# Expert stage of a two-layer trunk: branches placed in the engines' order, row pairs of 8 KB, and a rebuilt last sum

## The chip, the cores and the metric

The kernel runs on one core of one Trainium2 chip. The metric is the device time of one execution in microseconds. Three runs of the kernel before took 1338.13 to 1340.0 us, median 1339.05. All work is in float32; matrix products of "float32r" operands take one pass, those of float32 operands two instructions each in the trace.

## The reference

256 tokens of width 1024 pass an even layer (stick-breaking and differential attention, then a dense SwiGLU) and an odd layer (chunked band attention, then experts). The change touches the experts alone:

```python
logits = (t @ w_router).astype(F32)
top_val, top_idx = lax.top_k(logits, TOP_K)          # 2 of 8
gates = jax.nn.softmax(top_val, axis=-1)
combine = jnp.einsum('tk,tke->te', gates, jax.nn.one_hot(top_idx, N_EXPERTS, dtype=F32))
y = jnp.zeros_like(t)
for e in range(N_EXPERTS):                            # FF width 3584
    y = y + combine[:, e:e + 1] * swiglu(t, we_gate[e], we_up[e], we_down[e])
```

The weights of the eight experts are 8 x 3 x 1024 x 3584 floats, 352 MB.

## The kernel before

Everything up to the router (lines 203 to 790 and the setup from 1144 on) is the same in both kernels. After the router, each expert's rows are gathered by a product with a one-hot matrix (`dispatch`, `Rows.gather`, lines 888 to 914): the first 64 rows of an expert are its **main** rows, rows 65 to 96 its **further** rows. An expert whose count is above 64 is called crowded here; it needs the further rows too. In this input the experts 1, 3, 5 and 7 are crowded (their further products stand in the trace), 0, 2, 4 and 6 are not.

The 3584 columns of an expert are worked off in chunks of 512, 1024, 1024 and 1024 (line 793). For a chunk, `main_cols` (line 916) multiplies the 64 main rows by the gate and then by the up weights, two column halves at a time on the two 64-column halves of the array; `over_cols` (line 926) does the same for 32 further rows, with four column groups on the array's four 32-column parts. `swiglu` evaluates on ScalarE and VectorE, `turn` transposes the activations, `main_down` and `over_down` (lines 946 and 957) multiply by the down weights into sums that last over the expert. At its end `Scatter` splits the sums in a high and a low part (`split_from`), spreads them back to the tokens by a one-hot product (`halves`, `add_over`) and adds them, weighted, to `yx`; the last expert stores `yx`.

The weights arrive in pieces of 1 MB, one DMA each, issued by SyncE (line 801): 42 pieces an expert, four with rows of 2 KB (chunk 512), the others with rows of 4 KB, the down rows as two rows of 4 KB from different halves of the piece. A ring of 19 buffers holds them (7 `raw`, 6 `rawb`, 5 `w`, 1 `hTl`). `feed.more(n)` asks for n new pieces where n old ones have been used; in the chunk loop it stands behind the branch that holds the further products of gate and up (line 1099) and behind the one of the down rows (1111, 1120).

The further products stand in a branch, `arm` (line 1035, `tc.If` at 1041): eight an expert, one for gate and up of each chunk together, one for the down rows of each. All five engines pass every branch. An engine that skips one waits there until its own earlier work is done and then counts up its semaphore for what it left out.

The order on TensorE, ScalarE and VectorE is the traced order, written by `Ordered` (lines 840 to 857) between `begin` and `end`. `arm` ends an order ahead of the branch and begins one behind it, so the branch itself is in no order and the scheduler places it. The product banks: two for gate and up (`mm`), one shared in halves by the further gate and up (`gu`), one for the main down sum, two for the further down sums, two for transposes.

Of the kernel before, what the change touches and what calls it, by code (L numbers as in the profile page):

```python
# [44 lines left out]
DYN = True  # L45
# [3 lines left out]
def kernel(ctx: ExitStack, tc: tile.TileContext, A: dict, out: bass.AP):  # L49
# [27 lines left out]

    def raw_tile():
        pool, tag = ring[0]
        ring.rotate(-1)  # L80
        return pool.tile([P, 4, 512], F32, name=tag)
# [96 lines left out]

    @contextmanager
    def in_order():  # L180
# [8 lines left out]
        for i in traced[start:]:  # L189
            if i.engine in (EngineType.PE, EngineType.Activation, EngineType.DVE):  # L190
                if i.engine in last:
                    tc.add_manual_dep(i, last[i.engine], mybir.DependencyInfo(
                        mybir.DependencyClass.NoSync, mybir.DependencyReason.DATA), reason="in order")
                last[i.engine] = i.name
# [598 lines left out]
    CHUNKS = [(0, 512)] + [(c, 1024) for c in range(512, FFE, 1024)]  # L793

    def cols_piece(w, c0, n, k):

        nk = 2048 // n

        def load():
            r = raw_tile().rearrange("p a b -> p (a b)").rearrange("p (k c) -> p k c", c=n)  # L800
            nc.sync.dma_start(r, w[k * P:(k + nk) * P, c0:c0 + n].rearrange("(kb p) c -> p kb c", p=P))
            return r
        return load

    def rows_piece(w, r0):

        return cols_piece(w, 0, D, r0 // P)

    def pieces_of(e):

        for c, (c0, n) in enumerate(CHUNKS):
            for w in (eg[e], eu[e]):
                for k in range(0, KB, 2048 // n):
                    yield cols_piece(w, c0, n, k)
            if c:
                p0, pn = CHUNKS[c - 1]
                for r in range(p0, p0 + pn, 2 * P):
                    yield rows_piece(ed[e], r)
        c0, n = CHUNKS[-1]
        for r in range(c0, c0 + n, 2 * P):  # L820
            yield rows_piece(ed[e], r)
# [18 lines left out]
    class Ordered:  # L840


        def begin(self):
            self.bb = nc.cur_bb
            self.before = self.bb.bb.instructions[-1] if self.bb.bb.instructions else None

        def end(self):
            assert nc.cur_bb is self.bb
            traced = self.bb.bb.instructions
            start = next((k + 1 for k in reversed(range(len(traced))) if traced[k] is self.before), 0)  # L850
            last = {}
            for i in traced[start:]:
                if i.engine in (EngineType.PE, EngineType.Activation, EngineType.DVE):
                    if i.engine in last:
                        tc.add_manual_dep(i, last[i.engine], mybir.DependencyInfo(
                            mybir.DependencyClass.NoSync, mybir.DependencyReason.DATA), reason="in order")
                    last[i.engine] = i.name

    order = Ordered()

    with ExitStack() as ph:
# [4 lines left out]

        slots = act.tile([P, 2, P], F32, name="slots")
        nc.gpsimd.iota(slots[:, 0].rearrange("p (g s) -> p g s", g=2), pattern=[[0, 2], [1, MAIN]], base=0,
                       channel_multiplier=0, allow_small_or_imprecise_dtypes=True)
        nc.gpsimd.iota(slots[:, 1].rearrange("p (g s) -> p g s", g=GROUPS), pattern=[[0, GROUPS], [1, OV]], base=MAIN,  # L870
                       channel_multiplier=0, allow_small_or_imprecise_dtypes=True)
        slots = slots.rearrange("p a b -> p (a b)")
# [12 lines left out]
        yx = act.tile([P, T, D], F32, name="yx")  # L885
        aos = act.tile([P, 2, 1024 // GROUPS], F32, name="aos")

        def dispatch(e):

            dt = act.tile([P, T, 2 * P], F32R, name="disp")  # L890
            dx = act.tile([P, T, CAP], F32, name="dispx")
            for t in range(T):
                nc.vector.tensor_scalar(dx[:, t], slots[:, MAIN:MAIN + CAP], pos[:, t, e:e + 1], selx[:, t, e:e + 1],
                                        op0=OP.is_equal, op1=OP.mult)
            for t in range(T):
                nc.vector.tensor_scalar(dt[:, t], slots, pos[:, t, e:e + 1], sel[:, t, e:e + 1],
                                        op0=OP.is_equal, op1=OP.mult)
            return dt.bitcast(F32), dx
# [17 lines left out]
        def main_cols(o, rows, tiles, n):  # L916

            h, kb = n // 2, 0
            for r in tiles:
                for i in range(2048 // n):  # L920
                    for k in range(2):
                        mm(o[k * MAIN:(k + 1) * MAIN, 0:h], rows.xg[:, kb, 0:MAIN], r[:, i, k * h:(k + 1) * h],
                           kb == 0, kb == KB - 1)
                    kb += 1

        def over_cols(o, rows, tiles, n):
            h, kb = n // GROUPS, 0
            for r in tiles:
                for i in range(2048 // n):
                    for k in range(GROUPS):  # L930
                        mm(o[k * OV:(k + 1) * OV, 0:h], rows.xg[:, kb, MAIN:CAP], r[:, i, k * h:(k + 1) * h],
                           kb == 0, kb == KB - 1)
                    kb += 1

        def swiglu(a, g, u, w):
            nc.scalar.activation(a[:, 0:w], g[:, 0:w], AF.Silu)  # L936
# [408 lines left out]
```

## Time and profile before

| | us |
|---|---|
| runs (3) | 1338.13, 1339.05, 1340.0 |
| profiled execution, its own time | 1338.82 |
| its span, first to last instruction | 1337.1 |
| TensorE busy | 1285.9 (96%) |
| VectorE, ScalarE busy | 388.2, 322.5 |
| DMA moved | 426.71 MB, 318 GB/s read over the span |
| expert stage, first product to last sum | 464.7 to 1327.5 |

The profile cuts the span in 40 slices of 33 us and gives for each the busy tenths of every engine and of the DMA engines. From slice 15 on the DMA engines are full (9) and TensorE is at 9 or 8; VectorE and ScalarE are nearly idle. TensorE's granted clock is full in all slices but the last. A row of the timeline or of the chain begins with the start and the duration in us; a bracket behind it gives the idle time before and what ended it.

### The profile page before, as it was taken

The numbers are of one execution on the slowest core, as the hardware profiler recorded it, in microseconds if no ns is written. First come the engines' busy times: TensorE is split into PE (matmuls) and PEld (weight loads), VectorE is DVE, ScalarE is ACT, GpSimd is POOL, SyncE is SP. The second block draws the span as 40 slices with busy tenths as digits, with TensorE's granted clock in tenths as the row PEclk, the third lists the DMA queues.
The fourth block names the chain that finished last, engine by engine and source line by source line (L and its number), as shares of the span: only waits on it lengthen the run. The fifth ranks groups of instructions, "written<-read, shape, count | busy, mean of one in ns | idle before, by whom it ended". The sixth has DMA issues, their size and how long they took to land. (4 is left out here: it accounts for less than half of the span.)

```text
span 1337.1 us, 19574 instructions
## 1 busy us (share of the span) xinstructions
PE 1285.9 (96%) x8137; PEld 695.2 (52%) x8137; DVE 388.2 (29%) x738; ACT 322.5 (24%) x593; POOL 10.8 (1%) x34
## 2 busy tenths in 40 slices
PE   9999999999999999999999999999899999989995
PEld 6777888888776833533443433433343344334331
DVE  6965554446788500100110100020010011011002
ACT  7675544445666400000000000000000000000000
POOL 0000000000000000000000000000000000000000
PEclk9999999999999999999999999999999999999998
DMA  9623555556464979999999999999999999999981
GB/s 347 226 73 127 179 194 183 176 175 205 137 202 144 410 292 408 402 409 408 401 408 408 401 408 408 403 407 408 407 396 409 409 394 408 408 386 408 409 346 36
DMA packets 132877, 426.71 MB, mean 319 GB/s; under 512 B 7184, under 2 KB 9872, under 8 KB 132752
## 3 DMA queue, kind: packets, MB, share of 16 engines
q1 hardware_dynamic: 131680, 422.80, 82.0%
q0 software_dynamic: 640, 2.10, 0.7%
q8 instruction: 88, 1.44, 0.4%
q14 instruction: 37, 0.30, 0.1%
q10 hardware_dynamic: 432, 0.07, 0.1%
HBM read 423.89 MB, written 1.05 MB: 318 GB/s over the span
## 5 line engine op out<-in xcount | busy, mean ns | idle before, releaser
L60 PE MATMUL mm<-w,hTh 128*128 128x512 f32 (+2 forms) x968 | 291.4, 444 | 1.5 <-DVE w L141 0.8
L60 PEld LDWEIGHTS mm<-w,hTh 128*128 128x128 f32 (+1 forms) x968 | 153.3, 176 | 63.1 <-issue 27.8
L141 DVE TENSOR_TENSOR w<-raw,w 128x1024 fp32r<-128x1024 f32 (+1 forms) x127 | 153.9, 1214 | 91.0 <-ACT w L140 90.6
L140 ACT ACTIVATE w<-raw 128x1024 fp32r<-128x1024 f32 (+1 forms) x127 | 133.5, 1052 | 86.8 <-PE mm L60 51.3
L60 PE MATMUL mm<-w,hTl 128*128 128x512 f32 x368 | 146.4, 398 | 0.0
L60 PE MATMUL za<-raw,hTh 128*32 128x256 f32 (+2 forms) x1200 | 122.6, 417 | 6.5 <-DMA raw<-in_od_we_down 4.5
L937 DVE TENSOR_TENSOR aos<-za,aos 128x256 f32<-128x256 f32 (+1 forms) x16 | 6.3, 392 | 326.5 <-ACT aos L936 326.5
L60 PE MATMUL za<-rawb,hTh 128*32 128x256 f32 (+2 forms) x896 | 98.0, 434 | 2.7 <-DMA rawb<-in_od_we_down 1.7
L937 DVE TENSOR_TENSOR a<-mm,a 128x512 f32<-128x512 f32 (+1 forms) x31 | 19.6, 631 | 250.2 <-PE mm L60 250.2
L60 PEld LDWEIGHTS za<-raw,hTh 128*32 128x32 f32 (+1 forms) x1200 | 51.3, 118 | 70.6 <-issue 50.3
L944 ACT ACTIVATE hTh<-tr 128x512 f32<-128x512 f32 (+1 forms) x32 | 17.4, 544 | 284.7 <-PE tr L943 284.7
L60 PE MATMUL mm<-raw,hTh 128*64 128x512 f32 (+1 forms) x432 | 83.5, 526 | 1.9 <-DMA raw<-in_od_we_up 1.8
L60 PE MATMUL mm<-w,oTh 128*64 128x512 f32 (+2 forms) x344 | 79.2, 521 | 2.6 <-DMA w<-in_od_we_up 1.7
L60 PEld LDWEIGHTS mm<-w,hTl 128*128 128x128 f32 x368 | 69.4, 188 | 14.7
L60 PE MATMUL za<-w,hTh 128*32 128x256 f32 (+2 forms) x672 | 73.5, 441 | 2.1 <-issue 1.3
L60 PE MATMUL mm<-rawb,oTh 128*64 128x512 f32 (+1 forms) x360 | 70.7, 530 | 4.0 <-DMA rawb<-in_od_we_up 1.9
L60 PE MATMUL mm<-raw,oTh 128*64 128x512 f32 (+1 forms) x320 | 68.7, 565 | 2.5 <-DMA raw<-in_od_we_up 1.7
L60 PEld LDWEIGHTS za<-rawb,hTh 128*32 128x32 f32 (+1 forms) x896 | 39.8, 119 | 56.0 <-issue 40.6
L60 PE MATMUL mm<-rawb,hTh 128*64 128x512 f32 (+1 forms) x296 | 58.6, 539 | 1.8 <-DMA rawb<-in_od_we_gate 1.2
L60 PEld LDWEIGHTS mm<-raw,hTh 128*64 128x64 f32 x432 | 29.9, 136 | 47.6 <-issue 37.8
L60 PEld LDWEIGHTS mm<-w,oTh 128*64 128x64 f32 (+1 forms) x344 | 31.3, 146 | 39.6 <-issue 28.5
L60 PEld LDWEIGHTS za<-w,hTh 128*32 128x32 f32 (+1 forms) x672 | 29.8, 118 | 42.3 <-issue 32.0
(278 smaller groups left out, 1201.6 us busy)
## 6 DMA issues: line engine op xcount, KB each, us to landing
raw<-in_od_we_up SPq DMA_DIRECT2D x44, 1024.0 KB, 18.6
raw<-in_od_we_down SPq DMA_DIRECT2D x42, 1024.0 KB, 18.5
raw<-in_od_we_gate SPq DMA_DIRECT2D x40, 1024.0 KB, 18.5
rawb<-in_od_we_gate SPq DMA_DIRECT2D x38, 1024.0 KB, 18.6
rawb<-in_od_we_down SPq DMA_DIRECT2D x38, 1024.0 KB, 18.4
rawb<-in_od_we_up SPq DMA_DIRECT2D x32, 1024.0 KB, 18.6
w<-in_od_we_up SPq DMA_DIRECT2D x30, 1024.0 KB, 18.5
w<-in_od_we_gate SPq DMA_DIRECT2D x29, 1024.0 KB, 18.2
```

The costliest lines, as they stand in the source:

```text
L60: nc.tensor.matmul(o, lhsT, rhs, start=start, stop=stop, skip_group_check=True)
L140: nc.scalar.activation(hi[:, s], r[:, s], AF.Copy)
L141: nc.vector.tensor_tensor(lo[:, s], r[:, s], hi[:, s].bitcast(F32), op=OP.subtract)
L937: nc.vector.tensor_tensor(a[:, 0:w], u[:, 0:w], a[:, 0:w], op=OP.mult)
L944: nc.scalar.activation(dst[:, 0:w], pt[:, 0:w], AF.Copy)
```

## The change

1. `in_order` takes the place of `Ordered`. It stays open over the whole expert stage, and a branch instruction is put in the order of all three compute engines, where it was traced.
2. There is one branch behind each product: gate and up have one each, so 12 an expert (11 in expert 0, whose first gate product is made earlier, 13 in expert 7). `feed.more` follows each.
3. The gate's and up's banks are three in rotation (`banks`). The further product takes the bank that the next main product will take.
4. The further product of the 512 chunk is made in two groups of 256 columns in place of four of 128 (`groups`).
5. Down rows are loaded as `(p j) c -> p j c`: two neighbouring rows, 8 KB, to a partition. So that the rows match, the transposes read every second column of the activations (`turn`).
6. `turn` of the main activations stands in the middle of a main product, and the gather for the next expert behind the third down branch.
7. In the last expert the main and the further rows are summed in the same four banks (`finish`), behind all down products, and added once.
8. `yx`, the room for the split sums and `dT` are made at the end of expert 0; the activations and further activations have one buffer each; dispatch compares in four smaller steps. The eight counts are read inside the order, all ahead of the first expert.

```diff
@@ in_order
+            branch = "Conditional" in type(i).__name__
+            for engine in COMPUTE if branch else (i.engine,):
+                if engine not in COMPUTE:
+                    continue
+                if engine in last:
+                    tc.add_manual_dep(i, last[engine], mybir.DependencyInfo(
                         mybir.DependencyClass.NoSync, mybir.DependencyReason.DATA), reason="in order")
+                last[engine] = i.name
@@ rows_piece
-        return cols_piece(w, 0, D, r0 // P)
+        def load():
+            r = piece().rearrange("p (j c) -> p j c", j=2)
+            nc.sync.dma_start(r, w[r0:r0 + 2 * P, :].rearrange("(p j) c -> p j c", j=2))
+            return r
@@ products
+        def groups(n):
+            w = max(256, n // GROUPS // 256 * 256 + (256 if n // GROUPS % 256 else 0))
+            return n // w, w
+        def main_cols(o, rows, tiles, n, between=None):
...
+                if between and kb == KB // 2:
+                    between()
         def over_cols(o, rows, tiles, n):
-            h, kb = n // GROUPS, 0
...
+            g, w = groups(n)
+            for kb, r in enumerate(rows_in(tiles)):
+                for k in range(g):
+                    mm(o[k * OV:(k + 1) * OV, 0:w], rows.xg[:, kb, MAIN:CAP], r[:, k * w:(k + 1) * w],
+                       kb == 0, kb == KB - 1)
+        def turn(a, np, w, dst, m):
...
+                    c, j = b + i // 2 * 256, i % 2
+                    nc.tensor.transpose(pt[:, i * P:i * P + np], a[0:np, c + j:c + 2 * P:2], ident[0:np, 0:np])
@@ Scatter
+            def finish(self, aT, dn, n, rv):
+                yy = [split_room() for _ in range(2)]
+                self.split()
+                with arm(rv):
+                    over_down(yo, aT, dn, n, False, True)
+                    for h in range(2):
+                        split_from(yy[h][:, 0], yy[h][:, 1], yo[h])
+                os = [[acc[0], acc[1]], [acc[2], bank("tr")]]
+                for t in range(T):
+                    self.main_sums(os[t], t, rv is not None)
+                with arm(rv):
+                    for t in range(T):
+                        for h in range(2):
+                            self.over_sums(os[t][h], yy[h], t, False)
+                for t in range(T):
+                    for k in range(2):
+                        self.add_to(t, k, os[t][k])
+                        s = slice(k * 512, k * 512 + 512)
+                        nc.sync.dma_start(out[t * P:(t + 1) * P, s], total[0][:, t, s])
@@ arm
-            order.end()
             with tc.If(rv > MAIN):
-                order.begin()
-                yield
-                order.end()
-            order.begin()
+                with in_order():
+                    yield
+        def banks(n, use=True):
+            found = [acc[(at[0] + i) % 3] for i in range(n)]
+            at[0] += n * use
+            return found
@@ expert, chunk loop
+                if not done:
+                    gt = feed.take(KB // max(1, 2048 // n))
+                    g = banks(m)
+                    main_cols(g, rows, gt, n, (lambda: turn_main(0)) if c == 1 else None)
+                a = act.tile([P, 1024], F32, name="a")
+                if not done:
+                    activate(a, g, n)
+                    with arm(rv):
+                        go, = banks(1, False)
+                        over_cols(go, rows, gt, n)
+                        if c == 1:
+                            turn_over(0)
+                        nc.scalar.activation(ao[0:og * OV, 0:ow], go[0:og * OV, 0:ow], AF.Silu)
+                    feed.more(len(gt))
                 if c == 0 and before:
                     before.add(0)
...
+                activate(a, u, n, True)
+                with arm(rv):
+                    uo, = banks(1, False)
+                    over_cols(uo, rows, ut, n)
...
+                    nc.vector.tensor_tensor(ao[0:og * OV, 0:ow], uo[0:og * OV, 0:ow], ao[0:og * OV, 0:ow], op=OP.mult)
+                feed.more(len(ut))
                 if c == 0 and before:
                     before.add(1)
...
                 if c:
+                    down(c - 1, False, lambda: turn_main(c), c)
+            if nxt:
+                nxt.gather(range(0, 4))
+                nxt.gather(range(4, 8))
+            down(len(chunks) - 1, True)
```

## Rows read from the trace of the kernel before

**Rows 1.** The page, span in 40 slices: TensorE and DMA in tenths, GB/s moved

```profile
PE   9999999999999999999999999999899999989995
DMA  9623555556464979999999999999999999999981
GB/s 347 226 73 127 179 194 183 176 175 205 137 202 144 410 292 408 402 409 408 401 408 408 401 408 408 403 407 408 407 396 409 409 394 408 408 386 408 409 346 36
```

**Rows 2.** The chain that ended last: start, duration, what

```profile
1204.96 18.12 DMA w<-in_od_we_up
...
1225.32 7.04 PE za L60 x128
...
1326.91 0.61 DVE yx L998
```

**Rows 3.** Windows, one per expert 0 to 7: columns in the first line

```profile
core 0: us, PE busy (x) PEld busy (x) DVE busy (x) ACT busy (x) POOL busy (x), PEclk, DMA share, GB/s
464.70:545.98 81.28, 79.10 (x396) 30.98 (x396) 6.44 (x18) 4.84 (x9) 0.00 (x0) 1.00 0.91 358
545.98:670.36 124.38, 123.06 (x1068) 52.95 (x1065) 13.93 (x25) 9.27 (x20) 0.00 (x0) 1.00 1.03 407
670.36:758.93 88.57, 83.58 (x429) 32.41 (x427) 8.25 (x15) 5.33 (x10) 0.00 (x0) 1.00 1.03 406
758.93:886.73 127.80, 124.03 (x1068) 52.75 (x1066) 13.92 (x25) 9.27 (x20) 0.00 (x0) 1.00 1.03 406
886.73:977.77 91.04, 84.21 (x429) 32.21 (x427) 8.25 (x15) 5.33 (x10) 0.00 (x0) 1.00 1.02 404
977.77:1107.24 129.47, 125.82 (x1068) 53.29 (x1066) 14.02 (x25) 9.27 (x20) 0.00 (x0) 0.99 1.02 404
1107.24:1197.27 90.03, 83.97 (x428) 32.18 (x425) 8.25 (x15) 5.84 (x11) 0.00 (x0) 1.00 1.02 402
1197.27:1327.60 130.33, 123.55 (x1041) 50.16 (x1041) 15.20 (x24) 9.30 (x21) 0.00 (x0) 0.99 0.81 321
```

**Rows 4.** Windows of the expert stage where the transfers slow down

```profile
470.00:480.00 10.00, 9.22 (x42) 2.96 (x40) 0.13 (x1) 0.98 (x2) 0.00 (x0) 1.00 0.12 36
1190.00:1200.00 10.00, 8.61 (x48) 3.25 (x46) 0.69 (x1) 0.60 (x1) 0.00 (x0) 1.00 0.96 339
```

**Rows 5.** Timeline, SyncE and TensorE at the first branch

```profile
461.72 0.42 SPq L801 DMA_DIRECT2D hTl<-in_od_we_up  x1
469.71 0.42 DVE L1077 TENSOR_TENSOR a<-mm,a 128x256 f32<-128x256 f32 x1 [3.06 <-ACT a L1076]
478.31 0.37 SPq L801 DMA_DIRECT2D raw<-in_od_we_up  x1
478.96 4.91 PE L60 MATMUL mm<-rawb,oTh 128*64 128x512 f32 x21 [0.78 <-PEq L1041]
```

**Rows 6.** Windows, za products only: further products of chunk 512, chunk 1024

```profile
552.10:555.73 3.63, 3.63 (x128) 3.43 (x128) 0.00 (x0) 0.00 (x0) 1.00 1.02 406
571.21:578.26 7.05, 7.05 (x128) 4.06 (x128) 0.00 (x0) 0.00 (x0) 1.00 1.03 407
```

**Rows 7.** Timeline, expert 7: ScalarE evictions and TensorE behind one

```profile
1305.92 0.38 ACT L944 ACTIVATE oTh<-tr 128x256 f32<-128x256 f32 x1 [12.58 <-PE tr L943]
1306.25 0.60 ACT L944 ACTIVATE hTh<-tr 128x512 f32<-128x512 f32 x1
1306.90 1.51 PE L60 MATMUL za<-rawb,hTh 128*64 128x512 f32 x6 [0.75 <-ACT hTh L944]
```

**Rows 8.** Line 1041, the branches, and a usual wait behind a skipped one

```profile
L1041 PEldq COMPARE_BRANCH  x96: 70/176/4692, 473.8 to 1319.0; - x96
692.14 1.94 PE L60 MATMUL mm<-w,oTh 128*64 128x512 f32 x8 [0.16 <-PEq L1041]
```

**Rows 9.** Timeline, the end of expert 7

```profile
1315.05 0.60 ACT L247 ACTIVATE oTl<-zb 128x512 fp32r<-128x512 f32 x1 [8.20 <-PE zb L60]
...
1316.42 0.96 PE L60 MATMUL tr<-oTl,dT 128*128 128x512 f32 x3 [0.15 <-DVE oTl L248]
...
1319.92 1.94 PE L60 MATMUL za<-raw,hTh 128*64 128x512 f32 x8
...
1326.11 1.41 DVE L998 SCALAR_TENSOR_TENSOR yx<-tr,comb,yx 128x512 f32<-128x512 f32 x2 [0.89 <-PE tr L60]
```

**Rows 10.** Weight loads of the transposes in expert 1, by form

```profile
L943 PEld LDWEIGHTS tr<-ident,a 128*128 128x128 f32 x14 | 1.6, 140 | 3.2 <-issue 3.2
```

**Rows 11.** Windows, transfers of 2 KB rows, then of 4 KB rows

```profile
535.00:545.00 10.00, 9.69 (x59) 5.37 (x60) 1.12 (x2) 0.57 (x1) 0.00 (x0) 1.00 1.05 387
560.00:570.00 10.00, 10.00 (x49) 3.27 (x47) 0.00 (x0) 0.87 (x2) 0.00 (x0) 1.00 1.03 410
```

More of the change, by code (lines that the diff above doesn't have):

```diff
@@ L838, in take @@
             return [self.tiles.popleft() for _ in range(n)]
[L840 to L859, printed above, removed]
     with ExitStack() as ph:
@@ L926, in over_cols @@
         def over_cols(o, rows, tiles, n):
-            h, kb = n // GROUPS, 0
[L928 to L936, printed above, removed]
-            nc.vector.tensor_tensor(a[:, 0:w], u[:, 0:w], a[:, 0:w], op=OP.mult)
@@ L1008, in halves, with add_over @@
                 for k in range(2):
                     self.add_to(t, k, os[k])
[L1010 to L1025 removed]
+            def add_over(self, yy):
@@ new lines, in down @@
+            def down(c, final, between=None, turns=None):
+                n = chunks[c]
+                dn = feed.take(n // 256)
+                main_down(y, aTs[0][c % 2], dn, n, c == 0, final, between)
+                if final and last:
+                    s.finish(aTs[1][c % 2], dn, n, rv)
+                    return
+                if final:
+                    s.split()
+                    yy = act.tile([P, 2, 512], F32R, name="a")
+                with arm(rv):
+                    over_down(yo, aTs[1][c % 2], dn, n, c == 0, final)
+                    if turns is not None:
+                        turn_over(turns)
+                    if final:
+                        s.add_over(yy)
+                feed.more(len(dn))
@@ L1058, in expert @@
+            ao = aos
+            for c, n in enumerate(chunks):
                 done = first and not c
+                m = len(parts(n))
+                og, ow = groups(n)
                 gt = []
                 if not done:
[L1061 to L1067 removed]
+                    gt = feed.take(KB // max(1, 2048 // n))
[11 more added lines that the diff above has]
+                    feed.more(len(gt))
@@ L1112, in expert @@
-                was = a
-            n, i = CHUNKS[-1][1], (len(CHUNKS) - 1) % 2
-            dn = feed.take(n // 256)
-            main_down(s.y, aTs[0][i], dn, n, False, True)
-            s.split()
-            with arm(rv):
-                over_down(s.yo, aTs[1][i], dn, n, False, True)
-                s.add_over()
-            feed.more(len(dn))
-            if last:
-                for t in range(T):
-                    s.add(t, True)
+                if c == len(chunks) - 1:
+                    if not total:
+                        total.extend(sums())
+                    s.turn()
@@ L1293 @@
                 nc.vector.tensor_scalar(pos, pos, -float(CAP), None, op0=OP.add)
-                order.begin()
-                rows = Rows(0, rooms[0])
-                rows.gather(range(0, 4))
-                rows.gather(range(4, 8))
-                pieces = Pieces(p for e in range(NE) for p in pieces_of(e))
-                pieces.more(len(ring))
-                experts(rows, pieces, None, None)
-                order.end()
+                with in_order():
+                    rows = Rows(0, rooms[0])
+                    rows.gather(range(0, 4))
+                    rows.gather(range(4, 8))
+                    pieces = Pieces(p for e in range(NE) for p in pieces_of(e))
+                    pieces.more(len(ring))
+                    experts(rows, pieces, None, None)
 _BIG = ("ev_w_in", "ev_w_out", "ev_w_gate", "ev_w_up", "ev_w_down", "od_w_qkv", "od_w_out",
```

294 lines of the change are left out of this document (135 added, 159 removed).

## The prediction, made before the changed kernel ran

> **What bounds the kernel now.** I began with the slices. From slice 15 on the DMA engines are full and TensorE is at 9 or 8 tenths [rows 1]: two resources near their limit. The chain of waits says which one ends last: it follows transfers until 1223.07 us, and from there TensorE's products up to the last addition at 1326.91 [rows 2]. So the stream of weights binds until deep in the last expert, and then the products do. Cutting the stage by expert shows by how much [rows 3]. Expert 1 ran without waiting for the stream: 124.4 us for a crowded expert. A light one has about 83.6 us of products (83.58, 84.21, 83.97 busy). Against these prices the others lost: expert 2 5.0 us, 4 7.4, 6 6.4, 3 3.4, 5 3.6 (5.1 less 1.5 lost at the lower clock level: a mean granted clock of 0.99 is, by its rounding, 0.6 to 1.9 us, and I take a value in the upper half) and 7 3.4 (by its own tail, not in the rows of others). Sum 29.2 us of waiting for transfers. Without it a pair of experts would cost TensorE 124.4 + 83.6 = 208.0; the stream needs 84 pieces x 1.0486 MB at the 408 GB/s of the full slices [rows 1], or 215.9. The stream is the slower one by 8 us a pair.
>
> Where does the stream lose time of its own? In 470 to 480 it moved at 36 GB/s, and at 1190 to 1200 at 339 [rows 4]. The timeline gives the reason of the first: the nineteenth buffer is filled by an issue at 461.72 and the next issue comes at 478.31, since SyncE stands behind the first branch, which TensorE passes just ahead of 478.96 [rows 5]. That branch belongs behind the up product, whose eviction ended at 469.71 + 0.42. The scheduler had put it behind most of the next chunk's gate product.
>
> **The change, part by part,** against the profiled execution (1338.82 us, 0.23 under the median).
>
> *Branches in the order, one behind each product.* SyncE's first issue moves from 478.31 to about 470, so the hole of some 9 us shrinks to about 3: a gain of 6.2. Four later dips of the kind of 1190 to 1200 (17% of 10 us each, with their edges about 1 us) come from pieces freed in lumps behind two branches a chunk; with three they come smaller: about 4. The stream is then 10.2 us ahead. It no longer binds if TensorE's own path is later than it at each expert, and with the additions below it is: expert 7 would start at 1195 or later by the products (see the sum) and at 1197.27 - 10.2 = 1187 by the stream, while the 19 buffers allow a lead of 49 us. So the waits go: **-29.2**. What is late next is TensorE itself: its pair rises to 215.7, level with the stream's.
>
> *Further product of the 512 chunk in two groups.* Gate and up together are 128 instructions on four array parts: 3.63 us in chunk 512 and 7.05 in chunk 1024 [rows 6]. The first are 128 columns wide, the second, of chunk 1024, 256 wide, so 32 steps of four abreast take 0.22 each. The new form has 64 instructions of 256 columns for gate and up together, two abreast, so again 32 steps of 0.22, or 7.05 in place of 3.63: 3.4 for each of four crowded experts, **+13.6**. If two abreast run faster a step than four it is less, down to 0.
>
> *The bank shared by the next main product.* In a crowded expert the up product starts in the bank that the further gate product has just left, so TensorE stands until ScalarE has read it; three such meetings wait for SiLU of 128x256 (0.38, by the eviction of that size [rows 7]) and a gap of 0.1; chunk 1 has an eviction of turned rows ahead of it, 0.38 + 0.38 + 0.1 (before, that eviction's own gap of 0.75 on TensorE stood in expert 7 [rows 7]); chunk 0 is covered by the scatter products. 0.48 + 0.48 + 0.88 = 1.8, x 4 = **+7.2**. Ends: 0, if these products are long enough behind; 4.0 if each also waits for VectorE's multiplication.
>
> *More skipped branches.* Four more an expert. TensorE's usual gap behind a skipped one is 0.16 [rows 8]; that is 0.6. Skipping, ScalarE must pass the branch before the bank counts as free, which I put at the 0.78 that TensorE stood behind the first branch, where ScalarE was passing too [rows 5]; 0.78 - 0.16 on three chunks is 1.9. Together 2.5 in experts 2, 4 and 6, and 2.0 in expert 0, which also reads the eight counts in TensorE's order under the gather (0 to 2.5): **+9.5**. Ends: 0 for banks that are free, 4 x 0.78 = 3.1 a light expert, at the largest gap. What is queued behind these waits: on TensorE every later product, on SyncE the next eight or fewer issues (about 0.4 each [rows 5]), which the 49 us of buffers cover as long as they are full.
>
> *The end.* The gap of 0.75 [rows 7] goes, as turning moves into a product. The serial addition of the further rows, from 1315.05 to the next main product at 1319.92, goes: -4.9 [rows 9]. From the last main product's end (1319.92 + 1.94 = 1321.86) to the last addition's end (1326.11 + 1.41 = 1327.52) there are 5.66; the new tail has the two-step split (0.60 + 0.69), some 0.75 for the first bank's sums, and four additions of 0.7: 4.85, with the other sums beside the additions. -0.8, together **-6.4**. Bounds: -4.9 less all that the bank moves may add, say -3, and -8, if half of the split is covered too. The stores stand on SyncE behind the last weight issue, as now.
>
> *Costed at nothing.* Transposes of every second column: the weight loads of fourteen turned tiles take 0.14 us each, with 3.2 us idle ahead of them, 0.23 each [rows 10]. No row shows a strided one. Were they twice as long, the 28 of an expert would add 0.14 each, which that idle time covers; uncovered it is 3.9 an expert, 31 in all. I take 0. Rows of 8 KB: those of 2 KB moved 387 GB/s and those of 4 KB 410 [rows 11], or 2.71 and 2.56 us a piece, 0.15 less; half of that again, 0.075, over 112 down pieces makes 8.4 us, but for a stream that no longer ends last. Bounds for the stream: no gain, and 8.4; a loss is not excluded by a row, and would eat into the lead of 8 us. The dispatch in four steps, the extra passes on VectorE and ScalarE and the moved gather lie beside TensorE's products, both engines being busy for 5 to 15 of 80 to 130 us, and POOL for none [rows 3]. If a product had to wait for the dispatch, it would be about as long as the first gap, 0.78 [rows 5], once an expert. Behind the last addition 11.3 us remain, as before.
>
> Sum: -29.2 + 13.6 + 7.2 + 9.5 - 6.4 = -5.3. 1338.82 - 5.3 = 1333.5, and 0.23 to the median: **1334**. By expert: 83.3 for expert 0, 129.6 for a crowded one, 86.1 for a light one, so TensorE reaches expert 7 at 464.7 + 83.3 + 3 x 129.6 + 3 x 86.1 = 1195.1, or 1196.6 with the 1.5 of the lower clock level.
>
> The trace shows 96 branch passes on TensorE of 70 to 4692 ns, median 176, and a gap of 0.16 behind a skipped one [rows 8]; the sum goes by that gap. The Trainium skill, page "Runtime: NRT & Kernel Launch", section "Instruction fetch mechanics", says that a taken branch to a target outside the fetched window stops the engine until the target has been fetched, which speaks against four more skips an expert. By that rule each of these skips would cost more than the gap, which is rival C. The trace agrees with it as far as the 4692 ns go, and not in the gaps, which products already queued cover.
>
> **Rivals.** *B, faster by more, the waits for banks are hidden:* 0 in place of 16.7, TensorE's pair is 211.4 and the stream, 10.2 us ahead, sets the time as it did. Expert 7 starts at 1187.1 and takes 130.33 - 3.4 + 3.4 - 6.4 = 123.9; with 11.2 behind it that is 1322, and with seven eighths of the 8 KB gain 1315. For it: ScalarE and VectorE are idle most of the time [rows 3]. Against it: a product that reuses a bank cannot start ahead of its reader. Chance 0.20.
>
> *C, slower, by the branches:* the engine that skips an arm must get the instructions behind it, and TensorE's queue at the gate's new branch is too short to hide that. It decides from about 0.35 us more than forecast at each of 15 new gate branches of the light experts (5.3 us, the forecast's gain). At 0.78 more [rows 5] it is 1333.5 + 11.7 = 1345; at 0.62 more on all 47 branches of the light experts it is 1363. For it: passes of up to 4692 ns [rows 8]. Against it: most gaps in the trace are 0.16. Chance 0.18.
>
> *D, it does not do what it says:* SyncE waits as now, because an engine still reaches the branch late, the hole at 470 to 480 stays at some 36 GB/s, and the stream stays the bound up to expert 7: 1338.8 + 5.2 for its bank waits and wider product - 6.4 for the end = 1337.6, or 1337 to 1339. Against it: the branch is in all three engines' order; for it: SyncE's own issues are bound to none. Chance 0.20.
>
> **How the numbers follow.** The forecast has 0.42, B 0.20, D 0.20, C 0.18. The forecast's own range is 1330 to 1337. A measurement of this kernel tells 0.2% (2.7 us) from no change: faster is B and most of the forecast (0.57), same is D and the forecast's upper end (0.23), slower is C and a little (0.20). The range takes in most of B, all of the forecast and D and the lower part of C: 1321 to 1345.
>
> **What would show it.** In the profile after: the window 470 to 480 well above 36 GB/s and SyncE's first issue near 470; crowded experts at 129 to 130 and light ones at 86, with no wait for a transfer on TensorE after expert 1; the further products of chunk 512 at 7.05 for gate and up; waits of about 0.5 on ScalarE ahead of up products, and rows of 8 KB landing no later than now. Wrong if the chain still runs through transfers to the last expert (B or D, told apart by 470 to 480), or if gaps behind skipped branches near 0.8 add up (C); and the size of the tail is wrong if the last product-to-addition stretch is above 5.7.

## The result: 1.1% slower, with TensorE as the bound of the expert stage

The changed kernel takes 1354.01 us (median of 4 runs, 1352.91 to 1355.44), the kernel before 1339.53 beside it: ratio 1.0109, 95% interval [1.0098, 1.0121]. Its profiled execution spans 1352.1 us against 1337.1, so 15.0 us are to be explained. The forecast was 1334, a gain of 5; its range ended at 1345.

The page of the changed kernel, the span in 40 slices:

```profile
PE   9999999999999999999999999999999999999995
...
DMA  9623555555445999999999999999999999999931
GB/s 350 217 91 128 166 208 184 182 176 190 143 169 205 386 371 407 410 411 411 397 354 413 402 412 413 405 378 399 408 409 412 412 403 368 414 402 412 412 155 37
```

Against [rows 1]: TensorE has a 9 in every slice but the last. The transfers reach 412 to 414 GB/s where they run freely (408 before), and now fall back at places in mid-stage (354, 378, 368): the stream is held up by TensorE. The page's part 4, the chain of waits by engine (it reaches back to 1209.91 us), has no transfer in it, and some pieces of the chain in order of time follow it:

```profile
PE 9%; DVE 0%; ACT 0%; issue 0%; ACTq 0%; DVEq 0%
```

```profile
1237.68 0.36 ACT aos L1147
...
1238.09 7.09 PE za L59 x32
```

In [rows 2] it followed transfers until 1223.07. The piece at 1237.68 is one of the new waits, an up product standing until ScalarE has read the further gate product out of the bank. The windows by expert, columns as in [rows 3]:

```profile
465.65:549.91 84.26, 79.34 (x395) 31.30 (x395) 5.61 (x15) 7.21 (x12) 0.00 (x0) 1.00 0.97 383
549.91:682.15 132.24, 129.18 (x1002) 53.58 (x1003) 14.45 (x27) 9.91 (x21) 0.00 (x0) 0.99 1.01 403
682.15:771.09 88.94, 84.44 (x428) 33.55 (x427) 8.79 (x18) 5.31 (x10) 0.00 (x0) 0.99 1.00 394
771.09:902.70 131.61, 128.54 (x1004) 53.27 (x1004) 14.10 (x27) 9.81 (x21) 0.00 (x0) 1.00 1.01 402
902.70:990.60 87.90, 83.50 (x427) 33.09 (x427) 9.04 (x18) 5.21 (x10) 0.00 (x0) 1.00 1.02 404
990.60:1122.16 131.56, 128.50 (x1002) 53.24 (x1002) 14.05 (x27) 9.91 (x21) 0.00 (x0) 1.00 1.01 403
1122.16:1210.11 87.95, 83.55 (x428) 33.12 (x427) 9.09 (x18) 5.21 (x10) 0.00 (x0) 1.00 1.01 402
1210.11:1338.60 128.49, 125.36 (x978) 50.41 (x978) 12.50 (x20) 9.92 (x21) 0.00 (x0) 1.00 0.70 281
```

In the experts 3 to 6 a light expert (one that is not crowded) takes 87.9 and a crowded one 131.6, so a pair 219.5; the experts 1 and 2 take 132.2 and 88.9 at a mean granted clock of 0.99. Forecast were 86.1, 129.6 and 215.7. Waits for transfers are gone, as forecast: of TensorE's waits in the whole stage one alone is put down to a transfer, 1.45 us ahead of the first product at 465.65, and what stands there in TensorE's queue is the reading of the eight counts:

```profile
L1341 PEldq TENSOR_LOAD <-count x8: 300/307/490, 462.1 to 465.1; - x8
```

The stage from its first product to its last addition still grows from 862.8 us (464.70 to 1327.52) to 872.95 (465.65 to 1338.60). That is 10.1 of the 15.0. The first product comes 0.95 later, and from the last addition to the end of the span there are 13.5 us in place of 9.6: 3.9.

SyncE's first issue and the window 470 to 480 are as forecast, too; the window moved 36 GB/s before [rows 4]:

```profile
470.31 0.37 SPq L824 DMA_DIRECT2D raw<-in_od_we_up  x1
...
470.00:480.00 10.00, 8.27 (x38) 2.63 (x38) 0.42 (x1) 1.36 (x3) 0.00 (x0) 1.00 0.63 226
```

What the new waits are, by the waits of TensorE (what waits, for what, us in total, times, longest), first in the crowded expert 1, then in the light expert 2:

```profile
PE mm L59 <- ACT aos L1147: 1.1, 2, 0.6
PE tr L59 <- DVE a L255: 0.7, 1, 0.7
PE za L59 <- ACT aos L1147: 0.6, 1, 0.6
...
PE mm L59 <- ACTq L1075: 1.5, 2, 0.7
PE tr L59 <- PEq L1075: 0.8, 3, 0.3
PE za L59 <- ACTq L1075: 0.7, 1, 0.7
PE mm L59 <- PEq L1075: 0.7, 2, 0.4
PE za L59 <- PEq L1075: 0.6, 3, 0.3
PE tr L1007 <- PEq L1075: 0.2, 1, 0.2
```

`ACT aos` is the SiLU of the further gate product, three times 0.6. `ACTq L1075` is ScalarE's pass through a skipped branch, three times 0.7, where the up product takes the bank that the skipped arm (the branch's body) would have used. The `PEq` rows, 2.3 us, are TensorE's own passes through skipped branches.

### The profile page after: what moved, and what is told of

It is laid out like the page before. It is cut to its first block, busy times and chain, and to the rows that moved or that the text cites. A ratio compares the mean times of both kernels' runs of the same rounds, so it can differ in the third digit from the quotient of the medians.

```text
span 1352.1 us, 19378 instructions
## 1 busy us (share of the span) xinstructions
PE 1300.4 (96%) x7885; PEld 700.2 (52%) x7885; DVE 389.0 (29%) x750; ACT 324.8 (24%) x593; POOL 10.5 (1%) x33
## 5 line engine op out<-in xcount | busy, mean ns | idle before, releaser
L59 PE MATMUL mm<-w,hTh 128*128 128x512 f32 x736 | 240.0, 400 | 0.5 <-DVE w L143 0.5
L59 PEld LDWEIGHTS mm<-w,hTh 128*128 128x128 f32 x736 | 137.8, 188 | 32.6 <-issue 1.3
L1091 DVE TENSOR_TENSOR a<-mm,a 128x512 f32<-128x512 f32 (+1 forms) x22 | 13.6, 619 | 365.1 <-PE mm L59 169.7
L59 PE MATMUL mm<-raw,xg 128*32 128x256 f32 (+2 forms) x800 | 88.5, 428 | 1.5 <-ACT aos L1147 1.1
L59 PE MATMUL za<-raw,hTh 128*64 128x512 f32 x336 | 78.5, 598 | 0.5 <-PEq L1075 0.5
L59 PE MATMUL za<-rawb,hTh 128*64 128x512 f32 x304 | 69.9, 598 | 0.3 <-PEq L1075 0.3
L59 PE MATMUL mm<-rawb,xg 128*64 128x512 f32 (+2 forms) x440 | 67.8, 486 | 1.2 <-ACT aos L1147 1.2
L59 PEld LDWEIGHTS mm<-raw,xg 128*32 128x32 f32 (+1 forms) x800 | 38.8, 119 | 48.2 <-issue 28.6
L59 PE MATMUL za<-w,hTh 128*64 128x512 f32 x208 | 48.2, 599 | 0.3 <-PEq L1075 0.3
L59 PE MATMUL za<-raw,xg 128*32 128x256 f32 (+2 forms) x352 | 44.3, 449 | 2.1 <-ACT aos L1147 1.8
L59 PE MATMUL mm<-w,xg 128*32 128x256 f32 (+2 forms) x496 | 43.9, 416 | 1.1 <-ACT aos L1147 1.1
```

Source lines behind the costliest of these rows:

```text
L59: nc.tensor.matmul(o, lhsT, rhs, start=start, stop=stop, skip_group_check=True)
L1091: nc.vector.tensor_tensor(a[:, c:c + w], o[:, 0:w], a[:, c:c + w], op=OP.mult)
```

## The experiments

All were timed beside the kernel before on the same chip. Its median there was 1338.6 to 1339.6 us, so a difference between two kernels that ran on different chips is uncertain by about 1 us. Where it matters, a second figure is given, by the distances: the difference of what lies between each of the two and the kernel before beside it. Each run's name stands in brackets and what was expected of it stands behind its edit. Two readings recur. The position of the stream is the time at which so many of its 336 pieces were still to be moved, from the cumulated bytes of its queue. A pair is the time from the gather that precedes a crowded expert to the one two experts on, by the end of the gather's products.

**The wider product undone** (`four_groups`).

```diff
-            w = max(256, n // GROUPS // 256 * 256 + (256 if n // GROUPS % 256 else 0))
+            w = n // GROUPS
```

with the down rows and the transposes of the 512 chunk as before.

> The changed kernel, with the further product of the 512 chunk back in four groups of 128 columns (and, since the pairs of 256 columns don't fit that, the two down pieces of that chunk with rows of 4 KB). Theory 1, TensorE's own sequence sets the changed kernel's time, and the wider product is its largest added part: the further products of gate and up in that chunk fall from 3.6 us each to 1.8, 3.6 a crowded expert, 14 in all, so 1340 us (1338 to 1342). Theory 2, the stream or the way the weights are read sets it: no shorter than 1350 us, and the chain of waits shows transfers.

1339.98 us, ratio to the kernel before 1.0011 [1.0001, 1.0020]: 14.0 us less than the changed kernel (13.2 by the distances). In the changed kernel the further gate and up products of the chunk in expert 1 read, by windows:

```profile
553.51:557.09 3.58, 3.58 (x35) 1.78 (x33) 0.00 (x0) 0.38 (x1) 0.00 (x0) 1.00 1.03 412
561.35:564.93 3.58, 3.58 (x34) 1.78 (x32) 0.42 (x1) 0.00 (x0) 0.00 (x0) 1.00 1.02 423
```

7.16 for the two against 3.63 in [rows 6]: 3.5 a crowded expert, 14 in four. This term of the sum (13.6) held, and theory 1 with it.

**Banks of their own** (`own_bank`). The lines that change, but for one of expert 0:

```diff
-                    g = banks(m)
+                    g = [acc[0]]
-                        go, = banks(1, False)
+                        go = acc[2][:, 0:256]
-                u = banks(m)
+                u = [acc[1]]
-                    uo, = banks(1, False)
+                    uo = acc[2][:, 256:512]
```

> The changed kernel, with the gate, the up and the further products in banks of their own again (gate in the first, up in the second, the two further products in halves of the third), nothing else. Theory 1: the waits for ScalarE ahead of the up product (about 2.2 us in each crowded expert, of which the one behind the turned rows may stay) and TensorE's waits for ScalarE's passing of a skipped branch (2.2 us in each light one) go, less the 0.2 to 0.3 us that a skipped branch costs by itself: 12 to 15 us, so 1339 to 1342 us. Theory 2: 1352 to 1356 us, the banks are only where the waiting shows.

1339.43 us, 1.0002 [0.9993, 1.0012]: 14.6 less than the changed kernel (13.8 by the distances). The waits of TensorE from the gather ahead of the light expert 2 to the next one, whole:

```profile
PE tr L59 <- PEq L1075: 0.9, 3, 0.4
PE tr L59 <- DVE a L255: 0.8, 2, 0.7
PE mm L59 <- PEq L1075: 0.8, 3, 0.3
PE za L59 <- PEq L1075: 0.6, 2, 0.3
PE tr L59 <- ACT a L254: 0.5, 1, 0.5
```

`ACTq` and `ACT aos` are gone, in the other experts too but for one `ACTq` of 0.5 us. From gather to gather a crowded expert falls from 124.2 to 122.2 and a light one from 95.3 to 93.9. What is left for skipping twelve branches is 2.3 us (the `PEq` rows), 0.2 each. So of the 4.5 us of waits in a light expert of the changed kernel 2.2 stood at the shared bank, where the product had to wait for another engine's pass (1.4 of them are saved), and 2.3 at the skipping itself.

**The order alone** (`before_bound`). The kernel before, with the branches bound in the order as the change does it, eight an expert. Of the edit the part in `arm`:

```diff
-            order.end()
             with tc.If(rv > MAIN):
-                order.begin()
-                yield
-                order.end()
-            order.begin()
+                with in_order():
+                    yield
```

> The kernel before, with the branches alone put into the order of the three compute engines (still eight an expert, no other part of the change). Theory 1: SyncE's first issue moves from 478.3 to about 470 us, the hole in the stream shrinks by 6 us, the other dips by some more, no product gets longer; the waits for transfers in the experts 2 to 7 shrink, so 1329 to 1334 us. Theory 2, a bound branch makes the engines wait for each other by more than the stream gains: 1338 us or more.

1340.56 us, 1.0011 [1.0001, 1.0021]: no gain. SyncE's issues in this kernel's timeline, and two windows, columns as in [rows 3]:

```profile
470.62 0.37 SPq L806 DMA_DIRECT2D raw<-in_od_we_up  x1
471.12 14.83 SPq L806 DMA_DIRECT2D raw<-in_od_we_down  x2
486.05 1.08 SPq L806 DMA_DIRECT2D rawb<-in_od_we_down  x2
```

```profile
470.00:480.00 10.00, 9.53 (x48) 3.08 (x46) 0.42 (x1) 1.26 (x3) 0.00 (x0) 1.00 0.64 231
480.00:490.00 10.00, 9.68 (x46) 3.28 (x42) 0.69 (x1) 0.00 (x0) 0.00 (x0) 1.00 0.33 113
```

The issue moved from 478.31 [rows 5] to 470.62, just as theory 1 said. But only the pieces of the up product had come free there, and the next could not be issued until 486, behind the next branch of gate and up. The hole moved by ten microseconds and stayed as large: 310 pieces were left at 494.9 us, against 493.2 before. The first product starts 1.3 us later, at 465.96, since the eight counts are read inside the order here, too. Theory 2's time came, but not by its reason: the stream had gained nothing that the engines' waiting could take away.

**A branch behind each product, without the rest** (`before_twelve`). The same kernel, with the further gate product in a branch of its own and a request for pieces behind it.

```diff
                     main_cols(g, rows, gt, n)
+                    ao = aos[:, c % 2]
+                    go, uo = s.gu
+                    with arm(rv):
+                        if c == 1:
+                            turn(aos[:, 0], CHUNKS[0][1] // GROUPS, aTs[1][0])
+                        over_cols(go, rows, gt, n)
+                        nc.scalar.activation(ao[:, 0:ho], go[:, 0:ho], AF.Silu)
+                    feed.more(len(gt))
...
-                feed.more(len(gt) + len(ut))
+                feed.more(len(ut))
```

> The kernel before with the branches in the order and, beyond before_bound, a branch of its own behind each gate product (twelve an expert) with its own request for new pieces; banks, products, rows and end as before. Theory 1, it is the finer release of pieces that moves the stream, not the order: 310 pieces are left at about 488 us in place of 493 to 495, and TensorE, with no other cost than the four skipped branches, ends 5 to 8 us sooner than before_bound: 1332 to 1336 us. Theory 2, the branches cost TensorE what the stream gains: 1338 us or more.

1330.67 us, 0.9931 [0.9914, 0.9947]: 9.9 less than with the order alone (10.7 by the distances), a little below the range of theory 1. The same two views:

```profile
470.59 7.45 SPq L806 DMA_DIRECT2D raw<-in_od_we_down  x2
478.14 1.07 SPq L806 DMA_DIRECT2D rawb<-in_od_we_down  x2
```

```profile
470.00:480.00 10.00, 9.40 (x44) 3.18 (x46) 0.42 (x1) 1.26 (x3) 0.00 (x0) 1.00 0.70 245
480.00:490.00 10.00, 9.39 (x46) 3.21 (x43) 0.69 (x1) 0.30 (x1) 0.00 (x0) 1.00 1.03 414
```

The second group of pieces goes out at 478 in place of 486, and 310 are left at 487.0. TensorE's waits for transfers behind the first product fall from 21.7 to 9.5 us in all. So the stream's gain comes with the finer release of buffers; the order is worth nothing by itself. Whether the finer release would work without the order was not run.

**Gate and up in one branch again** (`one_branch_gate_up`), in the kernel with banks of its own (the arm behind the gate product moved into the one behind up, `feed.more(len(gt) + len(ut))`).

> The changed kernel with banks of their own, and the further products of gate and up in one branch behind the up product again (eight branches an expert, not twelve), all branches in the order. Theory 1, each skipped branch costs TensorE 0.2 to 0.3 us and the finer release of pieces is worth nothing where TensorE binds: four light experts lose four branches each, 3 to 5 us, so 1334 to 1337 us against 1339.4. Theory 2, it was the finer release of pieces that moved the stream forward by 5 us: with eight branches the slow stretch at 470 to 490 us comes back, TensorE waits for transfers, 1339 us or more.

1344.68 us, 1.0043 [1.0026, 1.0060]: 5.3 more than `own_bank`. 310 pieces are left at 494.6 again, as theory 2 says, but no wait of TensorE behind the first product is for a transfer, so neither theory gives the reason. It isn't a clean pair: both further products now stand side by side in two halves of one bank, and the second waits for ScalarE's reading of the first:

```profile
PE za L59 <- ACT aos L1158: 8.0, 16, 0.5
```

That wait (16 times 0.5) would explain the 5.3 by itself. The light experts 4 and 6, which it doesn't touch, take 93.5 against 93.9 us with four branches more. So a branch with its own bank costs 0.1 us there. Expert 2 takes 96.0, 2.0 more than in `own_bank`. There TensorE stands behind a skipped branch whose pass took 6196 ns, the longest of the run (a row of the timeline, then that of all passes: shortest/median/longest in ns):

```profile
703.56 2.79 PE L59 MATMUL za<-hTl,hTh 128*64 128x512 f32 x6 [2.07 <-PEq L1075]
...
L1075 PEldq COMPARE_BRANCH  x98: 70/174/6196, 467.5 to 1327.2; - x98
```

**Rows of 4 KB** (`rows_4k`). The changed kernel, with down rows and transposes as before. Of the edit the part in `turn`:

```diff
-                    nc.tensor.transpose(pt[:, i * P:i * P + np], a[0:np, c + j:c + 2 * P:2], ident[0:np, 0:np])
+                    src = a[0:np, b + i * P:b + i * P + P] if True else a[0:np, c + j:c + 2 * P:2]
+                    nc.tensor.transpose(pt[:, i * P:i * P + np], src, ident[0:np, 0:np])
```

> The changed kernel, with the down rows in pieces of two rows of 4 KB as before and the transposes reading neighbouring columns, nothing else. Theory 1: the stream isn't what the changed kernel waits for, so 1353 to 1355 us. Theory 2, reading every second column slows the transposes, or the 8 KB rows the transfers: under 1350 us, with shorter weight loads of the transposes or fewer waits for transfers.

1349.42 us, 1.0080 [1.0063, 1.0097]: 4.6 less than the changed kernel (3.8 by the distances). Theory 1 missed it. The weight loads of the transposes by form, the changed kernel first, then this one:

```profile
L956 PEld LDWEIGHTS tr<-ident,a 128*128 128x128 f32 x112 | 15.8, 208 | 26.0 <-issue 26.0
```

```profile
L960 PEld LDWEIGHTS tr<-ident,a 128*128 128x128 f32 x112 | 11.7, 141 | 26.0 <-issue 26.0
```

Reading every second column lengthens a load from 141 to 208 ns. The idle time ahead of the loads, 26.0 us, is the same in both kernels, so it covers nothing of this. The time of the transposes, each from its start to the next instruction's, falls from 3.02 to 2.69 us in a light and from 5.36 to 4.70 in a crowded expert: 0.33 x 4 + 0.66 x 4 = 4.0 of the 4.6. The stream itself is faster with 8 KB: 42 pieces in 107.8 us (294 to 252 left in the changed kernel) against 108.7 (the same here), and all fourteen kernels agree: 107.8 to 107.9 with 14 of the 42 pieces in rows of 8 KB, 108.0 to 108.2 with 12, 108.7 to 108.9 with none. TensorE simply did not wait for it.

**Two edits together** (`own_and_four`): banks of their own and four groups.

> The changed kernel with both of the edits that gained 14 us each: banks of their own, and four groups in the 512 chunk. Theory 1, TensorE's sequence alone sets the time: both gains add, 1339.4 - 14 = 1325 us. Theory 2, with TensorE's pair of experts at 212.7 us (122.2 - 3.4 + 93.9) against 215.6 of the stream (84 pieces at 2.567 us), the stream takes over: waits for transfers return on TensorE in the light experts, and the gain is 2 to 6 us smaller than the sum, so 1327 to 1332 us.

1326.68 us, 0.9913 [0.9897, 0.9930]. The two gains taken together give 1325.4, so it lies 1.3 above their sum (0.7 by the distances), which does not decide between the theories. The traces lean to the second. The first two pairs take 212.4, below the stream's 215.6, so its lead melts, and TensorE waits for transfers again, 2.4 us in all behind the first product, most of it in the last two experts:

```profile
PE mm L59 <- DMA rawb<-in_od_we_gate: 1.5, 2, 0.7
```

> As own_and_four, with all down rows in pieces of two rows of 4 KB and transposes of neighbouring columns. Theory 1, TensorE alone sets the time there: 4 us shorter than own_and_four, by the transposes alone. Theory 2, the stream has taken over: a piece costs 2.588 us in place of 2.567 (108.7 against 107.8 us for 42), 1 us an expert, so 3 to 7 us longer than own_and_four.

(`own_four_4k`: the same, with `rows_4k`'s edit) 1331.96 us, 0.9952 [0.9935, 0.9968]: 5.3 longer, of which TensorE's waits for transfers account for 3.9 (6.3 against 2.4 behind the first product). Here, with the stream the slower one, 8 KB rows are worth more than the transposes cost. Theory 2 holds.

**The old end** (`old_end`).

```diff
-                if final and last:
-                    s.finish(aTs[1][c % 2], dn, n, rv)
-                    return
```

and the main sums added and stored behind the loop.

> The changed kernel, with the last expert ended as the others are and as before: the further sums added inside the last branch, then the main sums added and stored. Theory 1: the shared sums save 5 us up to the last addition, but the four stores then all come at the end, where the last of them lands 6.5 us after the last addition against 2.6 before, which gives back 4: so 1354 to 1357 us. Theory 2, the forecast's: the new end is worth its full 6 us, 1359 to 1361 us.

1356.76 us, 1.0141 [1.0124, 1.0158], as theory 1 says: the new end is worth 2.8 us net (3.7 by the distances), not the 5.7 that the forecast put on this part (its 6.4 without the 0.75 for the moved turning, which this run keeps). TensorE's last stretch falls by the 4.9 that was summed (139.0 to 134.1 from the end of the last gather to the start of the last product), and up to the last addition's end it is 4.7. The tail behind the last addition is 13.5 us in the changed kernel, 12.1 here and 9.6 in the kernel before. The stores show in the transfers, the window from 1336 to 1347 of the changed kernel in 40 slices, busy tenths of the DMA engines:

```profile
DMA  0000229940299504899995340000101000000210
```

Their last packet ends 6.5 us after the last addition; in the kernel before, where half of the output goes out earlier, 2.6 after. But in `old_end` it ends 2.7 after, too, and the tail is still 12.1. So late stores account for at most 1.4 of the 3.9 us. The other 2.5 come with a part of the change that `old_end` keeps; which one stays open.

> As own_and_four, but the end sums, adds and stores the first 128 tokens before the second 128. Theory 1, the stores that all come after the last sums make the tail of 12 to 13.5 us behind the last addition: with two stores out earlier the tail falls to 10 to 11 us and the run by 1 to 3 us, to 1324 to 1326. Theory 2, the tail has another cause (what the engines do behind the last branch): the same 1326 to 1328 us.

(`end_by_halves`: `own_and_four` with `finish` changed to sum, add and store the first 128 tokens ahead of the second) 1325.35 us, 0.9892 [0.9875, 0.9908]. Against `own_and_four` that is 1.3 us less (2.3 by the distances), with intervals that overlap: not decided. The tail of 10 to 11 us that theory 1 asked for did not come; it is 12.0 against 12.3.

**Even and odd columns written apart** (`written_apart`). Added to `own_and_four`: ScalarE and VectorE write the activations in the order in which the transposes read them.

```diff
-                    nc.scalar.activation(a[:, c:c + w], o[:, 0:w], AF.Silu)
+                    nc.scalar.activation(apart(a[:, c:c + w], n), pairs(o[:, 0:w], n), AF.Silu)
```

(`apart` is `rearrange("q (b j p) -> q b p j")`, `pairs` is `"q (b p j) -> q b p j"`, and so for VectorE and the further rows.)

> As own_and_four, but ScalarE and VectorE write the activations with even and odd columns apart, so that the transposes read neighbouring columns while the down rows keep their 8 KB. Theory 1, the strided reads cost TensorE 0.33 us in a light and 0.66 in a crowded expert, three quarters of it here, and TensorE still sets the time: 2 to 4 us under own_and_four (1322.5 to 1325 us). Theory 2, the stream has taken over there: 0 to 1 us under it, with more waits for transfers.

1326.74 us, 0.9904 [0.9887, 0.9920]: not told apart from `own_and_four`. The transposes fall to 2.69 us in a light and 3.98 in a crowded expert (2.94 and 4.45 in `own_and_four`), and expert 6 then takes 96.5 us in place of 94.6, waiting for transfers: theory 2.

> Both edits of written_apart and end_by_halves. Theory 1: their gains add, 1320 to 1324 us. Theory 2: neither gains, 1325 to 1328 us.

(`apart_and_halves`) 1324.70 us, 0.9889 [0.9872, 0.9905]. This is the lowest median of all, 1.1% below the kernel before and 2.2% below the changed one. It lies between the two theories (up to 1324, and from 1325), and neither of its two edits is shown to gain by itself.

## Why the prediction was wrong

**The step that failed** is "What is late next is TensorE itself: its pair rises to 215.7, level with the stream's". Measured it is 219.5, 4 us above the stream's 215.6. That TensorE would be late next was right; what its pair would cost was not. By this the stream's lead bought nothing beyond the waits removed, and each microsecond that the sum left out of TensorE's work counted in full. Point by point:

- *Waits for transfers, -29.2: too large.* For light experts I took TensorE's busy time (83.6) as the time without waiting. The waits of the kernel before put only 3.7 of expert 2's 5.0 idle us on transfers and 1.0 on its skipped branches:

```profile
PE za L60 <- DMA rawb<-in_od_we_down: 1.7, 3, 0.6
PE mm L60 <- DMA raw<-in_od_we_up: 1.1, 2, 0.6
PE za L60 <- DMA raw<-in_od_we_down: 0.7, 1, 0.7
PE tr L60 <- PEq L1041: 0.5, 1, 0.5
PE mm L60 <- PEq L1041: 0.3, 2, 0.2
PE mm L60 <- DMA w<-in_od_we_up: 0.2, 1, 0.2
PE za L60 <- PEq L1041: 0.2, 1, 0.2
```

  Over the experts 2, 4 and 6 it is 13.6, where I had booked 18.8. The base of a light expert was low by a third of the difference, 1.7. The base of a crowded one held: 131.6 less 3.5 (two groups), 1.7 (bank), 0.7 (strided reads) and 1.1 (turns) is 124.6.
- *The mechanism of the stream's gain was half right.* SyncE's first issue moved as forecast, but 310 pieces were left no sooner with that alone (494.9 against 493.2). The finer release brings 310 left to 487 or 488; it was worth 9.9 us in the kernel before, where TensorE waited for transfers.
- *The two groups, +13.6: right* (14.0 by the run).
- *The shared bank, +7.2, and the branches in light experts, +9.5: near.* The waits were foreseen almost row by row: 1.7 us of `ACT aos` in a crowded expert (1.8 in the sum), 0.7 for each `ACTq` (0.78 in the sum). Separate banks give back 14.6; the crowded experts 2.0 each, the light ones 1.4. What was left is 0.2 per skipped branch.
- *Strided transposes, at 0: wrong*, 4.0 us by the trace, 3.8 to 4.6 by the times. The bound of twice the load lay above what was measured (208 against 141 ns), but I took the idle time ahead of the loads as cover, and the lengthening reached TensorE's time all the same, 0.33 us in a light and 0.66 in a crowded expert. (The rows show 14 such loads in a light expert and 22 in a crowded one, not 28.)
- *More branches in crowded experts, not in the sum.* In `own_and_four`, without bank waits, the main products of a crowded expert take 74.6 us against 74.0 in expert 1 before, and the further ones of gate and up 25.3 against 24.8 (each instruction from its start to the next one's): 1.1 more, with twelve turns between two kinds of products in place of eight. That is 4.4 us in four. Two pairs of runs take the turns apart from the rest. In `before_twelve`, which adds four turns to `before_bound`, the further products of expert 1 take 25.3 against 24.8 and the main ones 74.0 against 73.8. In `own_bank` the main ones take 74.6 against 74.1 in `one_branch_gate_up`. So at least 0.7 of the 1.1 comes with the turns. In the changed kernel the further products of gate and up in a chunk of 1024, now apart, show it, 7.25 in place of the 7.05 of [rows 6]:

```profile
573.20:576.86 3.66, 3.66 (x67) 2.05 (x65) 0.00 (x0) 0.60 (x1) 0.00 (x0) 1.00 1.04 412
584.90:588.49 3.59, 3.59 (x67) 1.98 (x65) 0.69 (x1) 0.00 (x0) 0.00 (x0) 1.00 1.04 428
```

  The Trainium skill, page "TensorEngine Tiling (Array Packing)", section "Key Properties", says that a change of the tiling mode drains TensorE, which would fit; no row here shows the drain itself.
- *The end, -6.4: oversized.* Up to the last addition the new end gains 4.7 us of the 5.7 that the sums and the shorter tail of products were to give. And what lies behind the last addition, which I had put down as unchanged ("11.3 us remain, as before"), took 3.9 back.
- *Expert 0, +2.0: 3.9* with the later first product. The reading of the counts was put at 0 to 2.5 us; TensorE stands 1.45 us for it.

The misses of a pair are 1.7 for the base, 1.0 for the strided reads and 1.1 for the turns: 3.8, as measured (219.5 - 215.7). Three pairs make 11.4; with 1.8 in expert 7 (0.66 + 1.1), 1.9 in expert 0 and 3.9 at the end it is 19.0 of the 20.0 us between 1334 and 1354. The 1.0 that the end fell short up to the last addition is the rest.

Of the rivals, B (the waits hidden) and D (nothing moves) did not come. C gave the right sign by the wrong cause: it asked for up to 0.78 us more than the forecast at skipped branches, for what an engine must fetch. TensorE's passes of the branches in the changed kernel are

```profile
L1075 PEldq COMPARE_BRANCH  x145: 70/174/445, 467.9 to 1335.5; - x145
```

at most 445 ns, in place of the 4692 of [rows 8]. Arms with one product each keep the passes at 445 or below in all eleven kernels that have them; in the three whose arms hold gate and up together the longest takes 3420 to 6196 ns, and in one of these it left 2.1 us uncovered, as shown above. So a pass that TensorE's queue did not hide, as C describes it, was seen, but not in the changed kernel; that fetching instructions takes the time is not shown. The Trainium skill, page "Runtime: NRT & Kernel Launch", section "Instruction fetch mechanics", lets a taken branch out of the fetched window stall for its target. These rows do not bear it out for arms as short as these; the long passes over the longer arms would fit it.

The range failed because costs put at nothing (4.0 for the strided reads, 3.9 for the tail) or not seen (4.4 for the turns) came together: 12.3 us, more than its 11 above the forecast.

## What to carry to other kernels

Before an engine's idle time is called waiting for one thing, take the rows of its waits: busy time is not the time without that wait. When a change removes a wait and adds small work to the engine that is nearly as late, sum the new pace of that engine over the repeated unit, here a pair of experts, and compare it with the other resource: 4 us in 216 decided. A bank or buffer that is handed from a conditional arm to the next product makes a skipped arm cost another engine's pass, 0.7 us here; with a buffer of its own the arm costs 0.1 to 0.2 us.

## What the runs showed of the hardware

- A weight load of a transpose that reads every second 4-byte element takes 208 ns against 141 for neighbouring ones. The Trainium skill, page "Advanced Engine Details and Errata", section "SBUF Cachelines", asks for at least two hits on a line of 16 bytes to absorb the latency of an access; a step of 8 bytes has two. The measurement differs: it costs 48% more here.
- Row pieces of 8 KB for a third of the stream moved 42 pieces in 107.8 us against 108.7 with 4 KB throughout.
- TensorE's pass of a skipped branch took at most 445 ns where an arm held one product, and up to 6196 ns where it held two. The two branches at the end of the changed kernel, which skip a whole second pass over the experts, took 3429 and 5652 ns. That the length is the reason is not shown.
